# The queries of four heads, moved from the head loop to the seven-product stage by way of DRAM

## The chip, the cores and the metric

The kernel runs on one core of a Trainium2 chip. The metric is the device time of one execution in microseconds (us): 1060.2 us is the median of three runs of the kernel before (1059.62 to 1060.6). The profile shown here comes from one further execution, which took 1058.51 us, 1056.7 us of it between its first and its last instruction (the span).

## The reference, cut to what matters

One layer with three parallel branches, merged by gates, then a feed-forward part. 640 tokens (512 sample, 128 prompt), model width 1024. All branches and gates take their inputs from one projection z = h @ w_in. The change concerns the first 512 columns of z, `zq`, from which the queries of four heads come.

```python
h = rms_norm(x, p['norm_mix']) * (1 + scale1) + shift1
z = h @ p['w_in']                       # 640 x 1024 times 1024 x 7168
zq, zf_f, zf_b, zi, zg, zu, zv, zp, zgate = jnp.split(z, offsets, axis=-1)
# hgrn2_mixer: 4 heads of 128
q = (jax.nn.silu(zq) * HG_DK ** -0.5)   # silu(x) = x * sigmoid(x)
f = lb + (1 - lb) * sigmoid(zf); k = 1 - f        # per direction d
o_d = gated linear recurrence of q, k, v = zi with decay f
o_hg = rms_norm(o_0 + o_1, norm_gain) * silu(zg)
merged = g_hg * (o_hg @ w_branch_hg) + g_sg * (o_sg @ w_branch_sg) + g_pool * (o_pool @ w_branch_pool)
```

## The kernel before, in words

Every projection is done in three matmuls for one product: both operands are split into a high and a low part (`split`, L124 to L127: ScalarE copies the high part, VectorE subtracts it to get the low part), and `mm3` (L193 to L198) multiplies high by high, high by low and low by high. The transposed input stands as `hx` (`h1h`, `h1l`), 8 slices of 128 features by 640 tokens, which are treated as two halves of 320. A block of z is 128 columns: 128 x 640 results.

TensorE's (PE's) instructions stand in program order; what the other engines and the DMA queue of SyncE (SP) run is put in order by a scheduler when the program is built, and each queue is then served strictly in that order.

There are two ways to make blocks of z.

The z stage (`z_pair`, L570) makes two blocks at a time from seven half-size products, in the manner of Strassen and Winograd: each of the seven is 4 slices x 3 matmuls of 128 x 320. It needs sums of the weights (`pair_forms`, L542) and of the inputs, which VectorE makes, and three evacuations and additions at the end. Each pair's weights are prepared during the pair before. The iterator `zpairs` (L538) says which columns come in which order: two pairs for the spatial branch (ZU), four pairs of gates, then pooling and more gates. Each pair's last product runs in the next pair (`pending`).

The head loop makes single blocks in the plain way (`z_cols`, L809, which calls `by_halves`, L798): for each half of the tokens 8 slices x 3 matmuls into one PSUM bank, of which there are three (`ps_mm`). `head_inputs` (L853) makes four such blocks for each head: the query Q (`silu`, L876), two forget gates (FF, FB) and the output gate (ZG). The weights of these blocks come in the order of `plan` (L170), two units ahead at least.

The recurrence of each head (`head`, L893) is a chain of small steps in which PE, VectorE and ScalarE take turns: a product of keys and queries (`scores`) for 32 tokens near each other, then seven levels, each with `scores`, a product on VectorE that updates `xq` in place, and another that updates `xk`, then transposes of the keys (`kt`), state updates (`upd`, then `sf` and `sb` on VectorE), the output product (`o`), its norm, and a transpose (`ot`) whose result is split into `oh`. These steps are strewn among the blocks' matmuls by a count of ticks: `tick()` (L208) is called after every two slices, that is after 6 matmuls, and a step that says `yield n` lets n ticks pass before the next one is written into PE's program:

```python
    LEVEL_TICKS = (3, 3, 3, 3, 2, 2, 2)
    ...
        yield 3              # before the first scores
        yield LEVEL_TICKS[n] # before the scores of level n
        yield 2              # before kt
        yield 2              # before upd
        yield 3              # before o
        yield 6              # before ot
```

That is 34 ticks for each head. A block in the head loop gives 8 ticks. The heads run one after another, each as soon as its inputs and the head before it are done. After the four heads' inputs `HG_ORDER` (L168) lists the rest: six gate blocks ("g", 8 ticks each), then the products of the branch's output with `w_branch_hg` ("b", which read `oh` of all four heads, head by head) mixed with two more gates. Ahead of the first "b" stands `drain()` (L1042), which writes all steps that are not yet in PE's program one behind the other.

Of the kernel before, what the change touches and what calls it, by code (L numbers as in the profile page):

```python
# [9 lines left out]
F32 = mybir.dt.float32  # L10
F32R = mybir.dt.float32r
I32 = mybir.dt.int32
AF = mybir.ActivationFunctionType
ALU = mybir.AluOpType
PSUM = bass.MemoryType.PSUM

P = 128
D = 1024
KD = D // P
TS, TP = 512, 128  # L20
T = TS + TP
NT = T // P
HALF = T // 2
# [7 lines left out]
NH = 4  # L31
# [4 lines left out]
OFF_Q, OFF_FF, OFF_FB, OFF_ZI, OFF_ZG, OFF_ZU, OFF_ZV, OFF_ZP, OFF_GATE = (  # L36
    0, 512, 1024, 1536, 2048, 2560, 3072, 3584, 4096)
# [28 lines left out]
def block_kernel(ctx: ExitStack, tc, x_prompt, x_sample, state, w_ada, w_in, w_bhg, w_bsg,  # L66
# [3 lines left out]
    nc = tc.nc  # L70
    ctx.enter_context(tc.manual_schedule(engines={mybir.EngineType.PE}))

    def pool(stack, name, bufs=1, space=None, side="left"):
        kw = {"side": side}
        if space is not None:
            kw = {"space": space}
        return stack.enter_context(tc.tile_pool(name=name, bufs=bufs, reuse_waits="tile", **kw))
# [7 lines left out]
    dram = ctx.enter_context(tc.tile_pool(name="dram", bufs=1, space=bass.MemoryType.DRAM))  # L85
# [67 lines left out]
    def cols_unit(w, c0, nk=KD):  # L153
        return (w, ((c0, P),), 0, nk)

    def rows_unit(w, n, q):
        return (w, ((n * 512, 512),), 2 * q, 2)

    def unit_parts(u):
        w, spans, k0, nk = u  # L160
        at, parts = 0, []
        for c0, n in spans:
# [5 lines left out]
    HG_ORDER = ([("g", j) for j in range(6)]  # L168
                + [("b", 0), ("b", 1), ("b", 2), ("g", 6), ("b", 3), ("b", 4), ("b", 5), ("g", 7), ("b", 6), ("b", 7)])
    plan = ([rows_unit(w_in, OFF_ZI // 512, q) for q in range(4)]  # L170
            + [cols_unit(w_in, c + h * P) for h in range(NH) for c in (OFF_Q, OFF_FF, OFF_FB, OFF_ZG)]
            + [cols_unit(w_in, OFF_GATE + j * P) if what == "g" else cols_unit(w_bhg, j * P, NH)
               for what, j in HG_ORDER]
            + [rows_unit(w_out, n, q) for n in range(2) for q in range(4)]
# [18 lines left out]
    def mm3(out, ws, xs, first, last, more=False):  # L193

        (wh, wl), (xh, xl) = ws, xs
        nc.tensor.matmul(out, lhsT=wh, rhs=xh, start=first, stop=False, skip_group_check=more)  # L196
        nc.tensor.matmul(out, lhsT=wh, rhs=xl, start=False, stop=False, skip_group_check=more)  # L197
        nc.tensor.matmul(out, lhsT=wl, rhs=xh, start=False, stop=last, skip_group_check=more)  # L198
# [4 lines left out]
    def later(n, fn):  # L203
        at = now[0] + n
        i = sum(d <= at for d, _ in due)
        due.insert(i, (at, fn))

    def tick():  # L208
        now[0] += 1
        while due and due[0][0] <= now[0]:  # L210
            due.pop(0)[1]()
# [106 lines left out]
    hx = (hpool.tile([P, KD, T], F32R, name="h1h"), hpool.tile([P, KD, T], F32R, name="h1l"))  # L318
    qscr = dram.tile([P, 2, HK, HALF], F32, name="qscr")
    vscr = dram.tile([P, NT, 512], F32, name="vscr")  # L320


    junk = spool.tile([P, D], F32, name="junk")
# [148 lines left out]
    zk = pool(zst, "zk", side="right")  # L472
# [25 lines left out]
    def q_tile():  # L498
        return ps_q.tile([P, 512], F32, tag="q", name="q")[:, 0:HALF]
# [30 lines left out]
    def branch_operand(pl, name):  # L530
# [4 lines left out]

    zpairs = iter([OFF_ZU, OFF_ZU + 2 * P] + [OFF_GATE + D + j * P for j in range(0, KD, 2)]  # L538
                  + [OFF_ZP + 2 * P, OFF_GATE + 2 * D, OFF_ZP]
                  + [OFF_GATE + 2 * D + j * P for j in range(2, KD, 2)])  # L540

    def pair_forms():  # L542
        c0 = next(zpairs, None)
        if c0 is None:
            yield None
        raws = [wraw(unit_parts(cols_unit(w_in, c)), KD) for c in (c0, c0 + P)]
        a11, a12, a21, a22 = (half_of(r, n) for r in raws for n in range(2))
        sm = zk.tile([P, HK * P], F32, tag="s", name="s", bufs=1)[:].rearrange("p (k c) -> p k c", k=HK)
        nc.vector.tensor_tensor(sm, a21, a22, op=ALU.add)
        nc.vector.tensor_tensor(a21, a21, a11, op=ALU.add)  # L550
        f = {}

        def put(ws, *names):
            for n, name in enumerate(names):
                f[name] = tuple(half_of(w, n) for w in ws)

        put(wsplit(raws[0]), "A11", "A12")
        nc.vector.tensor_tensor(a11, a11, sm, op=ALU.add)
        nc.vector.tensor_tensor(a12, a12, a11, op=ALU.add)
        ws = wpool.tile([P, 1024], F32R, tag="w", name="ws", bufs=WBUFS)[:].rearrange("p (k c) -> p k c", k=KD)  # L560
        f["s"] = half_of(ws, 0), half_of(ws, 1)
        split(*f["s"], sm)
        put(wsplit(raws[0]), "t", "u")
        yield f
        put(wsplit(raws[1]), "w", "A22")
        yield f
# [3 lines left out]
    def z_pair(done, extra=()):  # L570


        f = made.pop()
        extra = list(extra) + [lambda: None] * 2

        def product(bank, what, xs, first=False):
            for k in range(HK):
                mm3(bank, tuple(w[:, k, :] for w in f[what]), tuple(x[:, k, :] for x in xs),
                    first and k == 0, k == HK - 1, not first)
                if k % 2 == 1:  # L580
                    tick()

        a, b = q_tile(), q_tile()
        product(a, "A11", z11, True)
        product(b, "A12", z21, True)
        while pending:
            pending.pop(0)()
        g0, g1 = (zk.tile([P, T], F32, tag="u", name="z", bufs=7) for _ in range(2))
        ev = [zk.tile([P, HALF], F32, tag="ev", name="ev", bufs=3)[:] for _ in range(3)]
        nc.scalar.activation(ev[0], a, AF.Copy)  # L590
        c = q_tile()
        product(c, "s", zq1, True)
        forms = pair_forms()
        nc.scalar.activation(ev[1], c, AF.Copy)
        nc.vector.tensor_tensor(g0[:, 0:HALF], b, ev[0], op=ALU.add)
        product(a, "t", zq2)
        nc.scalar.activation(ev[2], a, AF.Copy)
        following = next(forms)
        extra[0]()
        product(c, "u", z22)  # L600
        if following:
            next(forms)
            made.append(following)
        nc.vector.tensor_tensor(g0[:, HALF:], c, ev[2], op=ALU.add)
        product(a, "w", zt3)
        nc.vector.tensor_tensor(g1[:, HALF:], a, ev[1], op=ALU.add)
        done(0, g0)
        extra[1]()

        def rest():  # L610
            product(a, "A22", zq4)
            done(1, g1, a)

        pending.append(rest)
# [26 lines left out]
    for g0 in (0, 2):  # L641
        def gelu_done(n, u, a=None, g0=g0):
            gelu(n, u, a)
            later(6, lambda: spatial(g0 + n, u))

        z_pair(gelu_done)

    def pool_out(g, pooled):
        px = px_tile()
        for h, to, z0, n in ((0, 0, ZA, HALF), (1, 0, ZA + HALF, TS - HALF), (1, TS - HALF, ZB, TP)):  # L650
            nc.tensor.matmul(px[:, h, to:to + n], lhsT=pw[:, g, :], rhs=pooled[:, z0:z0 + n], start=True, stop=True)
        nc.scalar.activation(halves(opl[0][:, g, :]), px[:, :, 0:HALF], AF.Copy, scale=par("pool_scale", g))
        nc.vector.scalar_tensor_tensor(halves(opl[1][:, g, :]), px[:, :, 0:HALF], par("pool_scale", g),
                                       halves(opl[0][:, g, :].bitcast(F32)), op0=ALU.mult, op1=ALU.subtract)
# [198 lines left out]
    def head_inputs(h):  # L853
        q = hz.tile([P, T], F32, tag="q", name="q", bufs=1)
        tot = hz.tile([P, 2, T], F32, tag="tot", name="tot", bufs=2)
        xk = hz.tile([P, 2, T], F32, tag="xk", name="xk", bufs=2)
        gz = hz.tile([P, T], F32, tag="gz", name="gz", bufs=2)

        def sig():
            return hz.tile([P, T], F32, tag="sig", name="sig", bufs=2)  # L860

        def forget(c0, d):
            at = slice(d * NH + h, d * NH + h + 1)
            sgs = [sig() for _ in range(2)]
            to = (tot[:, 1 - d, :], 1.0, lb[:, at]), (xk[:, d, :], -1.0, 0.0)

            def done(t, ps):
                for sg, (x, sign, bias) in zip(sgs, to):
                    nc.scalar.activation(sg[:, t], ps, AF.Sigmoid, scale=sign)
                if t.stop == T:  # L870
                    for sg, (x, sign, bias) in zip(sgs, to):
                        nc.scalar.activation(x, sg[:], AF.Identity, scale=lb1[:, at], bias=bias)

            z_cols(c0, done)

        def silu(c0, dst, scale):  # L876
            sg = sig()

            def done(t, ps):
                nc.scalar.activation(sg[:, t], ps, AF.Sigmoid)  # L880
                nc.vector.scalar_tensor_tensor(dst[:, t], ps, scale, sg[:, t], op0=ALU.mult, op1=ALU.mult)

            z_cols(c0, done)

        silu(OFF_Q + h * P, q, float(P) ** -0.5)
        if h == 0:
            nc.sync.dma_start(v[:], vscr[:])
        forget(OFF_FF + h * P, 0)
        forget(OFF_FB + h * P, 1)
        silu(OFF_ZG + h * P, gz, 1.0)  # L890
        return q, tot, xk, gz
# [659 lines left out]
    with tc.manual_schedule(engines={mybir.EngineType.Activation, mybir.EngineType.DVE, mybir.EngineType.Pool}):  # L1551
        ready = None
        for i in range(NT):
            for q, (c, ps) in enumerate(pss[i]):
# [3 lines left out]
                c = slice(512 + c.start, 512 + c.stop)  # L1558
# [97 lines left out]
```

## Time and profile before

| | |
|---|---|
| median of three runs | 1060.2 us (1059.62 to 1060.6) |
| profiled execution | 1058.51 us, span 1056.7 us |
| PE busy | 1034.5 us, 98% |
| VectorE (DVE) busy | 729.8 us, 69% |
| ScalarE (ACT) busy | 525.7 us, 50% |
| GpSimd (POOL) busy | 43.2 us, 4% |
| share of PE in the chain that ended last | 95% |

The stages on the time axis: inputs, norm and the first two projections to about 92 us, the z stage to about 303 us, the head loop with the six gates behind it to 520 us, the "b" products and gates to about 552 us, then the output projection and the feed-forward part. A matmul's duration in the trace overlaps with its neighbours', so the time of a matmul in a dense row is the distance between two starts. The granted TensorE clock has two levels, 1.00 (2.4 GHz) and 0.50 (1.2 GHz) in the profile's rows.

### The profile page before, as it was taken

The numbers are of one execution on the slowest core, as the hardware profiler recorded it, in microseconds if no ns is written. First come the engines' busy times: TensorE is split into PE (matmuls) and PEld (weight loads), VectorE is DVE, ScalarE is ACT, GpSimd is POOL, SyncE is SP. The second block draws the span as 40 slices with busy tenths as digits, with TensorE's granted clock in tenths as the row PEclk, the third lists the DMA queues.
The fourth block names the chain that finished last, engine by engine and source line by source line (L and its number), as shares of the span: only waits on it lengthen the run. The fifth ranks groups of instructions, "written<-read, shape, count | busy, mean of one in ns | idle before, by whom it ended". The sixth has DMA issues, their size and how long they took to land.

```text
span 1056.7 us, 19815 instructions
## 1 busy us (share of the span) xinstructions
PE 1034.5 (98%) x8230; PEld 964.2 (91%) x8230; DVE 729.8 (69%) x1119; ACT 525.7 (50%) x917; POOL 43.2 (4%) x111
## 2 busy tenths in 40 slices
PE   6999999999999999999999999999999999999997
PEld 4789999999999899898998899999999999888886
DVE  5486955697345665756465588999999998845634
ACT  5575644355225545543332366566666666634432
POOL 1030000000000000000000110000000000000201
PEclk9999999999999999999999999999999999999999
DMA  9964323232293544533236421222323223722202
GB/s 292 323 215 130 93 82 96 62 90 61 78 285 106 186 125 145 168 98 115 95 111 199 120 83 58 80 81 83 98 81 99 81 80 101 265 94 60 80 1 100
DMA packets 151770, 126.74 MB, mean 120 GB/s; under 512 B 4832, under 2 KB 132208, under 8 KB 151168
## 3 DMA queue, kind: packets, MB, share of 16 engines
q1 hardware_dynamic: 150960, 124.17, 38.4%
q8 instruction: 64, 1.05, 0.4%
q10 hardware_dynamic: 720, 1.31, 0.3%
q14 instruction: 26, 0.21, 0.1%
HBM read 114.96 MB, written 10.50 MB: 119 GB/s over the span
## 4 chain that ended last, share of the span: by engine, by line
PE 95%; DMA 1%; DVE 1%; ACT 1%; issue 1%; SPq 0%; POOL 0%; POOLq 0%; DVEq 0%; ACTq 0%
PE up L196 15%; PE up L198 15%; PE up L197 15%; PE mm L196 7%; PE mm L198 6%; PE mm L197 6%; PE q L196 5%; PE q L198 5%; PE q L197 5%; PE scores L912 2%; PE px L196 1%; PE px L198 1%; PE px L197 1%; PE ada L280 1%; PE zv L196 1%; PE zi L198 1%
## 5 line engine op out<-in xcount | busy, mean ns | idle before, releaser
L127 DVE TENSOR_TENSOR wl<-raw,wh 128x1024 fp32r<-128x1024 f32 (+1 forms) x105 | 123.9, 1182 | 91.7 <-ACT wh L126 34.4
L126 ACT ACTIVATE wh<-raw 128x1024 fp32r<-128x1024 f32 (+1 forms) x105 | 107.2, 1022 | 56.9 <-PE q L197 21.9
L196 PE MATMUL mm<-h1h,wh 128*128 128x320 f32 x384 | 123.5, 322 | 0.0
L198 PE MATMUL mm<-h1h,wl 128*128 128x320 f32 x384 | 118.7, 309 | 0.0
L197 PE MATMUL mm<-h1l,wh 128*128 128x320 f32 x384 | 118.6, 309 | 0.0
L197 PE MATMUL up<-wl,ah 128*128 128x512 f32 (+1 forms) x242 | 89.8, 371 | 0.0
L196 PE MATMUL up<-wh,ah 128*128 128x512 f32 (+1 forms) x242 | 89.7, 371 | 0.0
L198 PE MATMUL up<-wh,ah 128*128 128x512 f32 (+1 forms) x242 | 89.6, 370 | 0.0
L1198 ACT ACTIVATE wh<-raw 128x1024 fp32r<-128x1024 f32 x62 | 65.1, 1050 | 45.9 <-DVE raw L1189 43.6
L196 PEld LDWEIGHTS mm<-h1h,wh 128*128 128x128 f32 x384 | 72.1, 188 | 13.2 <-issue 12.8
L1203 DVE TENSOR_TENSOR wl<-raw,wh 128x1024 fp32r<-128x1024 f32 x62 | 75.6, 1220 | 8.4 <-ACT wh L1198 8.4
L197 PEld LDWEIGHTS mm<-h1l,wh 128*128 128x128 f32 x384 | 72.2, 188 | 0.0
L198 PEld LDWEIGHTS mm<-h1h,wl 128*128 128x128 f32 x384 | 72.1, 188 | 0.0
L126 ACT ACTIVATE ah<-act 128x512 fp32r<-128x512 f32 x88 | 35.9, 461 | 64.1 <-PE up L198 62.3
L127 DVE TENSOR_TENSOR ah<-act,ah 128x512 fp32r<-128x512 f32 x88 | 38.8, 487 | 32.5 <-ACT ah L126 32.5
L196 PE MATMUL q<-h1h,wh 128*128 128x320 f32 x192 | 59.7, 311 | 0.0
L198 PE MATMUL q<-h1h,wl 128*128 128x320 f32 x192 | 59.4, 309 | 0.0
L197 PE MATMUL q<-h1l,wh 128*128 128x320 f32 x192 | 59.4, 309 | 0.0
L196 PEld LDWEIGHTS up<-wh,ah 128*128 128x128 f32 x242 | 45.6, 189 | 7.8
L198 PEld LDWEIGHTS up<-wh,ah 128*128 128x128 f32 x242 | 45.6, 188 | 7.8
L197 PEld LDWEIGHTS up<-wl,ah 128*128 128x128 f32 x242 | 45.6, 189 | 7.8
L1278 DVE SCALAR_TENSOR_TENSOR acc<-u,pk,acc 128x643 f32<-128x643 f32 x48 | 42.4, 886 | 2.9 <-ACT acc L1272 2.0
(386 smaller groups left out, 2910.0 us busy)
## 6 DMA issues: line engine op xcount, KB each, us to landing
raw<-in_w_in SPq DMA_DIRECT2D x56, 512.0 KB, 4.3
raw<-in_ffn_up SPq DMA_DIRECT2D x44, 512.0 KB, 3.9
raw<-in_w_ada SPq DMA_DIRECT2D x32, 512.0 KB, 4.5
raw<-in_ffn_down SPq DMA_DIRECT2D x22, 512.0 KB, 3.7
raw<-in_w_ada SPq DMA_DIRECT2D x32, 256.0 KB, 6.1
raw<-in_w_out SPq DMA_DIRECT2D x8, 512.0 KB, 4.8
x2scr<-x SPq DMA_DIRECT2D x5, 512.0 KB
x<-x2scr SPq DMA_DIRECT2D x1, 2560.0 KB
```

Of the source, the lines that this page charges most:

```text
L126: nc.scalar.activation(hi, src, AF.Copy)
L127: nc.vector.tensor_tensor(lo, src, hi.bitcast(F32), op=ALU.subtract)
L196: nc.tensor.matmul(out, lhsT=wh, rhs=xh, start=first, stop=False, skip_group_check=more)
L197: nc.tensor.matmul(out, lhsT=wh, rhs=xl, start=False, stop=False, skip_group_check=more)
L198: nc.tensor.matmul(out, lhsT=wl, rhs=xh, start=False, stop=last, skip_group_check=more)
L280: nc.tensor.matmul(ps[tile_, 0:n // 4], lhsT=cs[:, k0 + k, :], rhs=w[:, g], start=(k0 + k == 0), stop=(k0 + k == KD - 1), tile_position=(0 ...
L912: nc.tensor.matmul(px[rows, i, to(g)], lhsT=ck[:, i * P + g * B:i * P + (g + 1) * B], rhs=rhs(i, g), start=True, stop=True, tile_position= ...
L1198: nc.scalar.activation(hi, src, AF.Copy)
L1203: nc.vector.tensor_tensor(lo, src, hi.bitcast(F32), op=ALU.subtract)
L1278: nc.vector.scalar_tensor_tensor(o, x, w, o, op0=ALU.mult, op1=ALU.add)
```

## The change

The four Q blocks leave the head loop. Two more pairs stand in `zpairs` behind the two ZU pairs; a new function `query_pair` makes them, with sigmoid, product and scale, and writes each finished 128 x 640 block to a scratch buffer in DRAM, `zscr`. In `head_inputs` a DMA from `zscr` into the tile `q` (one buffer) takes the place of `silu(OFF_Q ...)`. `plan` loses the four Q units. The ticks, `LEVEL_TICKS`, `HG_ORDER` and the place of `drain()` stay.

```diff
@@ plan
-            + [cols_unit(w_in, c + h * P) for h in range(NH) for c in (OFF_Q, OFF_FF, OFF_FB, OFF_ZG)]
+            + [cols_unit(w_in, c + h * P) for h in range(NH) for c in (OFF_FF, OFF_FB, OFF_ZG)]
@@ scratch
+    zscr = dram.tile([P, NH, T], F32, name="zscr")
@@ z stage
-    zpairs = iter([OFF_ZU, OFF_ZU + 2 * P] + [OFF_GATE + D + j * P for j in range(0, KD, 2)]
+    zpairs = iter([OFF_ZU, OFF_ZU + 2 * P, OFF_Q, OFF_Q + 2 * P] + [OFF_GATE + D + j * P for j in range(0, KD, 2)]
...
+    def query_pair(h0):
+
+        def done(n, z, a=None):
+            sign = (1.0, -1.0)[n]
+            if n:
+                nc.scalar.activation(z[:, 0:HALF], a, AF.Copy)
+            sg = zk.tile([P, T], F32, tag="u", name="sg", bufs=7)
+            nc.scalar.activation(sg[:], z[:], AF.Sigmoid, scale=sign)
+            nc.vector.scalar_tensor_tensor(z[:], z[:], sign * float(P) ** -0.5, sg[:], op0=ALU.mult, op1=ALU.mult)
+            nc.sync.dma_start(zscr[:, h0 + n, :], z[:])
+
+        z_pair(done)
+
+    for h0 in (0, 2):
+        query_pair(h0)
@@ head_inputs
-        silu(OFF_Q + h * P, q, float(P) ** -0.5)
+        nc.sync.dma_start(q[:], zscr[:, h, :])
```

On PE the end of the last head is where the program reads differently. Before, from the scores of level 5 on (`mm` is a block's product, `kt` the key transposes, `upd` the state updates):

```order
L912 MATMUL scores<-xq,ck 32x64 x20
L280 MATMUL ada<-raw,cs 32x256 x4
L196 MATMUL mm<-h1h,wh 128x320
L197 MATMUL mm<-h1l,wh 128x320
L198 MATMUL mm<-h1h,wl 128x320
...
L965 MATMUL kt<-ident,xk 128x128 x8
L196 MATMUL mm<-h1h,wh 128x320
L197 MATMUL mm<-h1l,wh 128x320
L198 MATMUL mm<-h1h,wl 128x320
```

In the changed kernel, from the scores of level 4 of the last head, the last step with a block's matmuls ahead of it:

```order
L198 MATMUL mm<-h1h,wl 128x320
L929 MATMUL scores<-xq,ck 32x32 x20
L280 MATMUL ada<-raw,cs 32x256 x4
L929 MATMUL scores<-xq,ck 32x64 x20
L280 MATMUL ada<-raw,cs 32x256 x4
L929 MATMUL scores<-xq,ck 32x64 x20
L280 MATMUL ada<-raw,cs 32x256 x4
L982 MATMUL kt<-ident,xk 128x128 x8
L990 MATMUL upd<-v,kt 128x128 x8
L1006 MATMUL o<-v,at 128x128
```

The 102 block matmuls that stood among these steps (12, 12, 12, 12, 18 and 36 of them from the scores of level 4 to `ot`) stand earlier in PE's program now; from the scores of level 4 to `ot` nothing stands between the steps. The other heads keep their 34 ticks.

On SP's queue the start of the head loop, before (`v` is the values' read, `sf` and `sb` are the first head's states):

```order
L134 DMA raw<-in_w_ada 128x1024 x3
L887 DMA v<-vscr 128x2560
L898 DMA sf_3482<-in_state 128x128
L899 DMA sb_3489<-in_state 128x128
L134 DMA raw<-in_w_in 128x8x128 x4
```

and in the changed kernel:

```order
L134 DMA raw<-in_w_ada 128x1024 x3
L902 DMA q<-zscr 128x640
L904 DMA v<-vscr 128x2560
L915 DMA sf_3687<-in_state 128x128
L916 DMA sb_3694<-in_state 128x128
L134 DMA raw<-in_w_in 128x8x128 x3
L902 DMA q<-zscr 128x640
L134 DMA raw<-in_w_ada 128x1024 x2
```

The first query comes in ahead of `v`, the second behind three weight units; each later one waits on the queue for the head before it to have read its own.

## Rows read from the trace of the kernel before

**Rows 1.** Page, part 1: busy us, share of the span, instructions.
```profile
PE 1034.5 (98%) x8230; PEld 964.2 (91%) x8230; DVE 729.8 (69%) x1119; ACT 525.7 (50%) x917; POOL 43.2 (4%) x111
```

**Rows 2.** Waits of PE, whole span: us in total, times, longest.
```profile
PE px L196 <- DVE z L716: 3.1, 2, 2.7
```

**Rows 3.** Stretches of z stage and last head: us, busy by engine, PEclk, DMA, GB/s.
```profile
130.00:292.00 162.00, 159.50 (x1081) 158.36 (x1079) 102.55 (x163) 68.78 (x112) 0.00 (x0) 1.00 0.28 82
...
471.00:517.00 46.00, 46.00 (x649) 41.15 (x648) 24.46 (x43) 17.98 (x40) 1.36 (x2) 1.00 0.33 105
```

**Rows 4.** Chain that ended last, z stage: start us, us, what.
```profile
109.14 1.11 PE px L629 x10
...
123.68 1.11 PE px L629 x10
```

**Rows 5.** PE timeline, end of the last head: start us, us, what.
```profile
489.36 0.31 PE L198 MATMUL mm<-h1h,wl 128*128 128x320 f32 x1
489.60 0.53 PE L912 MATMUL scores<-xq,ck 128*32 128x32 f32 x38
...
492.48 0.77 PE L912 MATMUL scores<-xq,ck 128*32 128x64 f32 x40
...
495.56 0.77 PE L912 MATMUL scores<-xq,ck 128*32 128x64 f32 x40
...
501.19 1.95 PE L973 MATMUL upd<-v,kt 128*128 128x128 f32 x16
...
505.62 0.38 PE L989 MATMUL o<-v,at 128*128 128x128 f32 x2
...
508.43 0.40 PE L196 MATMUL mm<-h1h,wh 128*128 128x320 f32 x1
...
513.80 0.71 PE L1004 MATMUL ot<-ident,o 128*128 128x128 f32 x5
514.26 0.39 PE L196 MATMUL mm<-h1h,wh 128*128 128x320 f32 x1
```

**Rows 6.** DVE timeline, the same stretch, idle before in brackets.
```profile
490.20 0.82 DVE L949 TENSOR_TENSOR xq<-xq,tot 128x640 f32<-128x640 f32 x1
...
502.28 1.11 DVE L976 SCALAR_TENSOR_TENSOR sf<-sf,tot,upd 128x128 f32<-128x128 f32 x3 [0.34 <-PE upd L973]
503.31 1.11 DVE L980 SCALAR_TENSOR_TENSOR sb<-sb,tot,upd 128x128 f32<-128x128 f32 x3
511.68 0.82 DVE L999 TENSOR_TENSOR o<-o,rso 128x640 f32<-128x640 f32 x1 [7.25 <-POOL rso L122]
...
514.54 0.88 DVE L1006 SCALAR_TENSOR_TENSOR og__5968<-ot,pk,gz 128x640 f32<-128x640 f32 x1 [0.88 <-PE ot L1004]
516.23 0.83 DVE L127 TENSOR_TENSOR ohgl<-og__5968,ohgh 128x640 fp32r<-128x640 f32 x1 [0.80 <-ACT ohgh L126]
```

**Rows 7.** ACT timeline, the same stretch.
```profile
496.40 0.70 ACT L944 ACTIVATE at<-scores 128x640 f32<-128x640 f32 x1 [0.29 <-PE scores L912]
497.13 1.37 ACT L947 ACTIVATE at<-near 32x160 f32<-32x160 f32 x4
499.19 1.09 ACT L967 ACTIVATE kt<-kt 128x512 f32<-128x512 f32 x2 [0.69 <-PE kt L965]
...
508.71 0.28 ACT L996 ACTIVATE o<-o 128x128 f32<-128x128 f32 x1 [3.93 <-PE o L989]
...
515.46 0.74 ACT L126 ACTIVATE ohgh<-og__5968 128x640 fp32r<-128x640 f32 x1 [0.96 <-DVE og__5968 L1006]
```

**Rows 8.** Page, part 5: the weights' low parts: busy us, mean ns, idle before.
```profile
L127 DVE TENSOR_TENSOR wl<-raw,wh 128x1024 fp32r<-128x1024 f32 (+1 forms) x105 | 123.9, 1182 | 91.7 <-ACT wh L126 34.4
```

**Rows 9.** Stretches at the program's end, where PE has finished: columns as in rows 3.
```profile
1049.00:1050.00 1.00, 0.33 (x3) 0.13 (x2) 0.89 (x3) 0.56 (x2) 0.00 (x0) 1.00 0.00 0
...
1051.50:1052.00 0.50, 0.00 (x0) 0.00 (x0) 0.10 (x1) 0.10 (x1) 0.36 (x1) 0.98 0.09 25
1052.00:1053.00 1.00, 0.00 (x0) 0.00 (x0) 0.65 (x1) 0.62 (x1) 0.00 (x0) 0.50 0.00 0
```

## The prediction

> **What bounds the kernel now.** I read the page's busy shares first: PE is busy for 98% of the span, no other engine for more than 69% [rows 1]. Then PE's waits: the whole list beyond the start and the tail holds one place that matters, 3.1 us before the head loop, where VectorE is late with a product [rows 2]. Then the stretches: the z stage keeps PE busy for 159.5 of 162 us, the last head for 46.00 of 46 [rows 3]. So before the change the time is PE's program, row after row; what leaves it is gained at full price, and what makes PE wait is lost at full price. Last the timelines of the last head on three engines [rows 5 to 7], since the diff leaves its ticks alone while it takes away the matmuls that the ticks count.
>
> **Part 1: PE's work.** Between the starts of two `px` groups of one z pair lie 123.68 - 109.14 = 14.54 us with two such groups of 1.11 us and the pair's 84 matmuls: 12.32 / 84 = 0.1467 us for one [rows 4]; the last head's pitch is the same. Four Q blocks are 4 x 48 = 192 matmuls, two pairs 2 x 84 = 168. 24 fewer: -3.5 us.
>
> What the pairs add elsewhere I cost at nothing. On VectorE a query pair has the sums and low parts of any pair, and two products of the size of the `og` row, 0.88 us each [rows 6]; it has no `px` product or branch weights. The stage has VectorE at 102.55 of 162 us and ScalarE at 68.78 [rows 3], and weights are made during the pair before. If that cover failed, PE would wait for about one low part a pair, 1.2 us [rows 8], so 0 to +2.4 us. I see no way to below nothing. The four writes to DRAM stand on SP ahead of later weight reads, and each waits for VectorE's product; those reads serve a pair that starts a pair, 12.3 us, later. I take 0, at worst the same 2.4 us.
>
> The read of `q` has a head's whole input time (24 ticks, over 21 us at 6 x 0.1467 each) to land before the first product that needs it. Each later one waits on SP until the head before has read its query; behind it stand weight reads of units that are at least two blocks of 7 us away. I take 0.
>
> **Part 2: the ticks.** A head needs 34 ticks. Before, its inputs gave 4 x 8 = 32: the heads start at ticks 33, 67, 101 and 135, the last ends at 169, and the drain comes at 4 x 32 + 6 x 8 = 176. Nothing is left to drain but a few ticks of slack. After, a head's inputs give 24: the heads start at 25, 59, 93 and 127, and the drain comes at 4 x 24 + 48 = 144, when the last head has done 17 of 34 ticks. Its steps due at 19, 21, 23, 25, 28 and 34 (scores of levels 5 and 6, `kt`, `upd`, `o`, `ot`) are written one behind the other. The 102 matmuls that stood between are done sooner, so they are not lost, but they no longer cover anything, and the first "b" product needs the last head's `oh`.
>
> How long is that chain bare? From the start of the level-4 scores (0):
> - VectorE first makes a low part whose buffer the block just ended has freed, 1.2 us [rows 8], then updates `xq`, 0.82 [rows 6], and hands over in 0.04 (from `og`'s end at 515.42 to `ohgh` at 515.46 [rows 6, 7]): level 5 at 2.05.
> - scores to next engine 0.84 (495.56 to 496.40 [rows 5, 7]), `xq` 0.86: level 6 at 3.75.
> - ScalarE: `at` starts at 4.6, the near copies 0.73 later, and take 1.37; half of the `kt` copies, 0.55 [rows 7]: `upd` at 7.25.
> - `sf` 1.09 after `upd`'s start, `sb` 1.03 later, 1.11 long [rows 5, 6]: 10.5.
> - `o`: 13 pieces in 508.43 - 505.62 = 2.81 us [rows 5]; two are done before `sb` is, eleven remain: 12.9.
> - squares 0.28 later, then 2.97 to the product with the norm (508.71 to 511.68), which hands to `ot` after 0.86 [rows 5 to 7]: 17.0.
> - `og` 0.74, `ohgh` 0.92, `ohgl` 0.77, and 0.87 to PE: 20.3.
>
> PE's own work in it: 514.26 - 489.60 = 24.66 us less 102 x 0.1467 = 14.96, so 9.7 us [rows 5], and ten matmuls of the first "b" half (heads 0 to 2 and one more), 1.5 us. The rest is idle: 20.3 - 9.7 - 1.5 = +9.1 us.
>
> Bounds for the unseen bare chain: without the low part in front, and with the `kt` copies ahead of the near copies, 17.7 us, idle 6.5; at most as long as it was with its matmuls between, 516.23 + 0.83 - 489.60 = 27.5 us, idle 16.3 [rows 5, 6]. I take 20.3, as each step has a row of its own size.
>
> **Part 3: the clock.** Between `o` and `ot` PE would stand for 4.1 us (12.9 to 17.0). At the program's end the granted clock is 1.00 until just before 1052, some 2.6 us after the last matmul, and 0.50 from there on [rows 9]; a wait of 2.7 us at 290 us did not bring it down [rows 2, 3]. So it probably falls once here. At 1.2 GHz `ot` (0.46 us, 513.80 to 514.26 [rows 5]) takes as long again, the ten matmuls still fit ahead of `ohgl`, and some of the following "b" products run at half speed until it rises: 0 to 3 us, I take +1.0 in all.
>
> The Trainium skill (TensorE: Matmul & The Clock Gate, section on HAM oscillation) says that waits between bursts of matmuls bring the clock back to half rate, and that each burst then starts slow. By that rule the term of 1.0 stands, and it speaks for the second rival below; without it the sum would be 1.0 us lower. The fall in the last rows agrees with it.
>
> **The sum.** -3.5 + 9.1 + 1.0 = +6.6 us. From the profiled execution's own 1058.5 us that is 1065.1; the median of the runs shown stands 1.7 us above that execution, and I put the change on the median: 1060.2 + 6.6 = 1066.8 us.
>
> **Rivals.**
> - *The clock is at half through most of the drain.* Between the steps PE does small products with gaps of 1 to 2 us, so the clock could go already at `kt`. Then `upd`, `o` and `ot` on the chain take twice as long (0.9, 2.4 and 0.5 us more) and some 3 us of "b" products too: about 5 us on top, 1072. For it: the fall in rows 9. Against: PE is dense until the level-4 scores, and none of those gaps is as long as the 2.7 us that left the clock alone. The page named above would allow it.
> - *Heads that hold their buffers (slower still).* The inputs now run ahead of the heads by ten ticks a head. The last head's `xk` is written at tick 80, and its buffer is freed by the second head's `kt`, at tick 82; behind that wait on ScalarE stand this head's second `kt` copy and the next block's sigmoids. Three PSUM banks let PE go on for eight ticks, so I cost it at 0; three such places at one 0.9 us tick each would give 1069.5.
> - *VectorE becomes the bound of the query pairs.* Then 2.4 us of the gain go: 1069.2. Against it is its load in the stage.
> - *The other side: the bare chain is nearly covered.* With VectorE and ScalarE free of block work, the last head's steps follow each other so fast that PE idles less than the 3.5 us saved; it decides from a chain of 14.7 us downward (9.7 + 1.5 + 3.5). At no idle at all the time is 1056.7. Against it: its own rows give 17.7 at least.
>
> **How the numbers follow.** Forecast 66%, its own range 1063 to 1070; half clock 13%; held buffers 10%; VectorE 5%; the chain covered 6%. A measurement of this kernel tells about 0.2% from no change, 2.1 us: slower means above 1062.3, faster below 1058.1. Slower holds the first four but for a small part of the forecast's lower edge: 0.89. Of the covered chain most gives faster: 0.05; same 0.06. The range that holds 8 in 10 goes from 1062.5, just under the short chain (1063.2 with no clock loss), to 1073, the long chain without a clock loss and the half clock.
>
> **What would show it.** Right: PE busy without a gap in the z stage, 24 fewer 320-column matmuls; `scores` rows of the last head's levels 4 to 6 within 4 us; a new PE wait of some 4 us before `ot` (for VectorE's `o`), ones of 1 to 3 us before `upd` and `o`, and one for `ohgl` at the first "b" product, 9 us together; a granted clock of 0.50 for a few us behind it. Wrong: no such waits; waits of PE between 92 and 130 us or at the heads' `scores`; or idle time on PE under 3.5 us between levels 4 and "b".

## The result, and the profile after

The changed kernel takes 1066.0 us (median of four runs, 1065.4 to 1066.47), the kernel before 1059.91 us in the runs beside it and those shown above (four, 1057.96 to 1060.6). The ratio is 1.006, with a 95% interval of 1.0047 to 1.0073: slower by 6.1 us. The profiled execution took 1065.4 us, 1063.6 of it span, 6.9 us more than the span before.

Busy shares, the first part of the page of the changed kernel; they answer to [rows 1]:

```profile
PE 1034.3 (97%) x8206; PEld 963.6 (91%) x8206; DVE 740.4 (70%) x1133; ACT 532.8 (50%) x925; POOL 43.0 (4%) x111
```

PE issues 24 matmuls fewer (8230 to 8206) and is busy as long as before. Either the matmuls saved nothing, or others take longer; the rows below show that it is the second. PE's waits over the whole span (us in total, times, longest), which answer to [rows 2]:

```profile
PE ot L1021 <- DVE o L1016: 4.0, 1, 4.0
...
PE px L196 <- DVE z L733: 2.3, 1, 2.3
PE scores L929 <- DVE xq L966: 1.9, 2, 1.1
PE upd L990 <- ACT kt L984: 1.4, 1, 1.4
...
PE o L1009 <- DVE sb L997: 0.9, 1, 0.9
```

The wait at `px` was there before. The other four are new, 8.2 us together, and all lie in the end of the last head. Here is that end on PE (start us, us, what, in brackets the idle time before); it answers to [rows 5]:

```profile
506.22 0.53 PE L929 MATMUL scores<-xq,ck 128*32 128x32 f32 x38
...
508.29 0.77 PE L929 MATMUL scores<-xq,ck 128*32 128x64 f32 x40 [1.07 <-DVE xq L966]
...
510.28 0.77 PE L929 MATMUL scores<-xq,ck 128*32 128x64 f32 x40 [0.79 <-DVE xq L966]
...
511.41 1.09 PE L982 MATMUL kt<-ident,xk 128*128 128x128 f32 x8
513.88 2.05 PE L990 MATMUL upd<-v,kt 128*128 128x128 f32 x16 [1.38 <-ACT kt L984]
...
517.27 0.49 PE L1009 MATMUL o<-sb,xq 128*128 128x128 f32 x2 [0.89 <-DVE sb L997]
...
519.61 0.39 PE L1006 MATMUL o<-v,at 128*128 128x128 f32 x2
524.00 1.33 PE L1021 MATMUL ot<-ident,o 128*128 128x128 f32 x5 [4.01 <-DVE o L1016]
524.98 0.61 PE L196 MATMUL mm<-ohgh,wh 128*128 128x320 f32 x1
...
525.66 0.47 PE L198 MATMUL mm<-ohgh,wl 128*128 128x320 f32 x1
525.93 0.47 PE L196 MATMUL mm<-ohgh,wh 128*128 128x320 f32 x1
...
527.94 0.64 PE L197 MATMUL mm<-ohgl,wh 128*128 128x320 f32 x1
...
529.97 0.33 PE L198 MATMUL mm<-ohgh,wl 128*128 128x320 f32 x1
530.14 0.31 PE L196 MATMUL mm<-ohgh,wh 128*128 128x320 f32 x1
```

The steps follow each other with nothing between. From `ot` on PE works at half pace: `ot` to the next matmul takes 0.98 us where it took 0.46 [rows 5], and the "b" products have a pitch of 0.27 us (525.66 to 525.93), where it is 0.147 at full speed. Stretches of the changed kernel (us, busy by engine, then PEclk, DMA share, GB/s), which answer to [rows 3] and, for the clock, to [rows 9]:

```profile
142.00:305.00 163.00, 163.00 (x1108) 162.36 (x1107) 106.41 (x163) 72.31 (x117) 0.00 (x0) 1.00 0.28 80
340.00:480.00 140.00, 140.00 (x1953) 125.44 (x1953) 86.81 (x140) 69.82 (x140) 3.53 (x4) 1.00 0.50 154
506.00:523.00 17.00, 9.86 (x196) 7.73 (x195) 7.57 (x18) 6.78 (x22) 1.28 (x2) 1.00 0.33 109
506.00:531.00 25.00, 16.86 (x225) 14.39 (x225) 10.60 (x22) 7.51 (x23) 1.36 (x2) 0.86 0.25 86
523.00:524.00 1.00, 0.00 (x0) 0.00 (x0) 0.82 (x1) 0.00 (x0) 0.09 (x1) 0.59 0.70 287
524.00:524.50 0.50, 0.50 (x3) 0.50 (x4) 0.00 (x0) 0.00 (x0) 0.00 (x0) 0.50 0.00 0
529.50:530.00 0.50, 0.50 (x4) 0.50 (x4) 0.00 (x0) 0.00 (x0) 0.00 (x0) 0.50 0.00 0
530.00:531.00 1.00, 1.00 (x8) 1.00 (x8) 0.00 (x0) 0.00 (x0) 0.00 (x0) 1.00 0.02 8
```

The z stage, now with the query pairs, keeps PE busy all the time, and so do the heads from 340 to 480 us. In the 25 us of the last head's end PE stands idle for 8.1. The granted clock is 1.00 through the four shorter waits, falls during the long one, some 3 us after the last `o` matmul, and is back at 1.00 by 530 us, after `ot` and 5 us of "b" products with hardly a pause.

VectorE in the same stretch, which answers to [rows 6]:

```profile
506.18 1.23 DVE L127 TENSOR_TENSOR wl<-raw,wh 128x1024 fp32r<-128x1024 f32 x1 [0.16 <-PE mm L197]
507.32 0.82 DVE L966 TENSOR_TENSOR xq<-xq,tot 128x640 f32<-128x640 f32 x1
...
523.12 0.82 DVE L1016 TENSOR_TENSOR o<-o,rso 128x640 f32<-128x640 f32 x1 [5.91 <-POOL rso L122]
525.37 0.88 DVE L1023 SCALAR_TENSOR_TENSOR og__6036<-ot,pk,gz 128x640 f32<-128x640 f32 x1 [1.42 <-PE ot L1021]
527.06 0.83 DVE L127 TENSOR_TENSOR ohgl<-og__6036,ohgh 128x640 fp32r<-128x640 f32 x1 [0.80 <-ACT ohgh L126]
```

The weight's low part does stand in front of the first `xq`, as the chain of the prediction had it, and `og` comes 1.37 us after the start of `ot` instead of 0.74. ScalarE (ACT) ahead of `upd`, which answers to [rows 7]:

```profile
511.84 1.37 ACT L964 ACTIVATE at<-near 32x160 f32<-32x160 f32 x4
513.23 1.09 ACT L984 ACTIVATE kt<-kt 128x512 f32<-128x512 f32 x2
```

The near copies do stand ahead of the `kt` copies, for 1.4 us, though PE waits for the latter alone.

### The profile page after: what moved, and what is told of

Read it like the earlier page. It is cut to its first block, busy times and chain, and to the rows that moved or that the text cites. A ratio compares the mean times of both kernels' runs of the same rounds, so it can differ in the third digit from the quotient of the medians.

```text
span 1063.6 us, 19823 instructions
## 1 busy us (share of the span) xinstructions
PE 1034.3 (97%) x8206; PEld 963.6 (91%) x8206; DVE 740.4 (70%) x1133; ACT 532.8 (50%) x925; POOL 43.0 (4%) x111
## 4 chain that ended last, share of the span: by engine, by line
PE 49%; DVE 1%; ACT 1%; issue 0%; POOL 0%; POOLq 0%; ACTq 0%
PE up L196 15%; PE up L198 15%; PE up L197 15%; PE mm L197 1%; PE mm L196 1%; PE mm L198 1%; PE up L1150 0%; ACT wh L1215 0%; ACT o L1013 0%; PE ot L1021 0%; DVE wl L1220 0%; POOL rso L122 0%; PE upd L990 0%; PE o L1009 0%; DVE sb L997 0%
## 5 line engine op out<-in xcount | busy, mean ns | idle before, releaser
L127 DVE TENSOR_TENSOR wl<-raw,wh 128x1024 fp32r<-128x1024 f32 (+1 forms) x107 | 126.3, 1183 | 86.1 <-ACT wh L126 39.2
L196 PE MATMUL mm<-h1h,wh 128*128 128x320 f32 x320 | 102.9, 322 | 0.0
L198 PE MATMUL mm<-h1h,wl 128*128 128x320 f32 x320 | 98.9, 309 | 0.0
L197 PE MATMUL mm<-h1l,wh 128*128 128x320 f32 x320 | 98.8, 309 | 0.0
L196 PE MATMUL up<-wh,ah 128*128 128x512 f32 (+1 forms) x242 | 89.6, 370 | 0.0
L196 PEld LDWEIGHTS mm<-h1h,wh 128*128 128x128 f32 x320 | 60.1, 188 | 11.9 <-issue 11.1
L196 PE MATMUL q<-h1h,wh 128*128 128x320 f32 x224 | 69.5, 310 | 0.0
L197 PE MATMUL q<-h1l,wh 128*128 128x320 f32 x224 | 69.2, 309 | 0.0
L198 PE MATMUL q<-h1h,wl 128*128 128x320 f32 x224 | 69.2, 309 | 0.0
L197 PEld LDWEIGHTS mm<-h1l,wh 128*128 128x128 f32 x320 | 60.2, 188 | 0.0
L198 PEld LDWEIGHTS mm<-h1h,wl 128*128 128x128 f32 x320 | 60.1, 188 | 0.0
L196 PEld LDWEIGHTS up<-wh,ah 128*128 128x128 f32 x242 | 45.6, 188 | 7.8
```

The lines of the kernel that those rows point to most:

```text
L127: nc.vector.tensor_tensor(lo, src, hi.bitcast(F32), op=ALU.subtract)
```

## The experiments

Each kernel was timed in turn with the kernel before; ratios are to that. The first two ask whether the loss has the place and the cause that the prediction gave it; then it is halved, and taken away in two ways; the last asks what the clock is worth.

**The pairs alone.** The heads still make their own queries, so that their ticks are those of before; the pairs' queries go to DRAM and are not read.

```diff
-            + [cols_unit(w_in, c + h * P) for h in range(NH) for c in (OFF_FF, OFF_FB, OFF_ZG)]
+            + [cols_unit(w_in, c + h * P) for h in range(NH) for c in (OFF_Q, OFF_FF, OFF_FB, OFF_ZG)]
-        nc.sync.dma_start(q[:], zscr[:, h, :])
+        silu(OFF_Q + h * P, q, float(P) ** -0.5)
```

Expected: 

> The first part of the change alone: the two query pairs are made in the z stage and written to DRAM, but the heads still make their own queries in the loop and do not read the pairs' (so 168 matmuls of 128x320 are done for nothing). The ticks are as in the kernel before. Theory (the pairs cost PE's work and nothing else, and the read by way of DRAM has no part in the loss): 1059.6 + 168 x 0.1467 = 1059.6 + 24.6 = 1084.2 us, no wait of PE in the z stage, none in the last head's end. Rival (VectorE or the writes hold PE up in the query pairs): 2.4 us more, 1086.7, with waits of PE between 115 and 150 us. Rival (the loss is not from the ticks but from the z stage or the transfer): 1090 or more.

Measured: 1083.43 us (four runs, 1082.23 to 1084.08) beside 1060.4; ratio 1.0212 (1.0197 to 1.0227), that is +22.5 us (20.9 to 24.1). Its stretches of the query pairs (their sigmoids run from 126 to 146 us) and of the last head's end:

```profile
112.00:142.00 30.00, 30.00 (x212) 30.00 (x211) 25.39 (x42) 17.32 (x26) 0.00 (x0) 1.00 0.36 109
...
516.00:545.00 29.00, 29.00 (x291) 27.78 (x291) 9.81 (x21) 9.95 (x28) 1.36 (x2) 1.00 0.22 72
```

VectorE is at 25.4 of 30 us in the query pairs, so it has little to spare there, but PE never waits for it. With the ticks back, the end of the last head has no wait. The sum of 24.6 us lies half a microsecond above the interval; the wait at `px`, 3.1 us before and 2.3 here, is more than that. The first part of the change costs PE its matmuls and no more than that. This kernel does not read the queries back; that the reads cost nothing is seen in the changed kernel, where PE has no gap from 340 to 480 us.

**The drain alone, in the kernel before.** Nothing of the queries is changed; three gate blocks stand ahead of the first "b" instead of six, so that the drain comes at tick 4 x 32 + 3 x 8 = 152, with the last head at tick 17 of 34, as in the changed kernel.

```diff
-    HG_ORDER = ([("g", j) for j in range(6)]
-                + [("b", 0), ("b", 1), ("b", 2), ("g", 6), ("b", 3), ("b", 4), ("b", 5), ("g", 7), ("b", 6), ("b", 7)])
+    HG_ORDER = ([("g", j) for j in range(3)] + [("b", 0), ("b", 1), ("b", 2)]
+                + [(what, j) for j in range(3, 8) for what in ("g", "b")])
...
-        if n == 6:
+        if n == 3:
             drain()
```

Expected: 

> The kernel before, queries in the head loop, with three gate blocks instead of six ahead of the drain (the other five follow among the b products): the drain comes at tick 152 with the last head at tick 17 of 34, as in the changed kernel, and the same PE work in all. Theory: the same waits of 8 us and the half clock behind them, with nothing saved: 1060 + 11 = 1071 us, 1069 to 1073. Rival A (pairs of the z stage or buffers make the loss, not the drain): 1060 to 1062.

Measured: 1070.32 us (four runs, 1068.68 to 1071.22) beside 1059.64; ratio 1.010 (1.0085 to 1.0115). Its waits of PE:

```profile
PE ot L1004 <- DVE o L999: 4.0, 1, 4.0
...
PE scores L912 <- DVE xq L949: 1.9, 2, 1.1
PE upd L973 <- ACT kt L967: 1.4, 1, 1.4
...
PE o L992 <- DVE sb L980: 0.9, 1, 0.9
```

These are the changed kernel's waits, to the tenth, in a kernel without the change, and here too the granted clock is 0.50 behind the longest (508 to 513 us). It lies 10.7 us above before (9.0 to 12.2), the changed kernel 6.1: the difference is the 3.5 us of matmuls that only the latter saves, within the intervals.

**Half the dose.** The changed kernel with seven gates ahead of the drain (tick 152; the last head is at tick 25 of 34).

```diff
-    HG_ORDER = ([("g", j) for j in range(6)]
-                + [("b", 0), ("b", 1), ("b", 2), ("g", 6), ("b", 3), ("b", 4), ("b", 5), ("g", 7), ("b", 6), ("b", 7)])
+    HG_ORDER = ([("g", j) for j in range(7)]
+                + [("b", 0), ("b", 1), ("b", 2), ("b", 3), ("b", 4), ("b", 5), ("g", 7), ("b", 6), ("b", 7)])
...
-        if n == 6:
+        if n == 7:
```

Expected: 

> The changed kernel with seven gate blocks ahead of the drain instead of six, and the seventh "b" where the seventh gate stood. The last head is then at tick 25 of 34 when the drain comes: the steps up to upd have their matmuls again, only o and ot are bare. Theory (the bare chain is the loss, step by step): the waits before scores and upd (1.9 and 1.4 us) go, those before o and ot (0.9 and 4.0 us) stay, so 1066.0 - 3.3 = 1062.7 us. On the clock: if the 4 us wait before ot alone brings it down, the granted clock is 0.50 behind it as in the changed kernel; if the row of shorter waits ahead of it was needed, it stays at 1.00 and the time is another 1 to 1.6 us lower, 1061.1 to 1061.7. Rival (one fixed price for any drain ahead of the head's end): no less than 1065.

Measured: 1062.91 us (twelve runs, 1061.26 to 1064.87) beside 1060.4; ratio 1.0025 (1.0014 to 1.0035). Two of its waits, and two of its stretches:

```profile
PE ot L1021 <- DVE o L1016: 3.9, 1, 3.9
...
PE o L1009 <- DVE sb L997: 0.9, 1, 0.9
```

```profile
526.00:527.00 1.00, 0.00 (x0) 0.00 (x0) 0.16 (x1) 0.00 (x0) 0.80 (x1) 0.90 1.07 451
...
532.00:533.00 1.00, 1.00 (x5) 1.00 (x5) 0.41 (x1) 0.00 (x0) 0.00 (x0) 0.50 0.00 0
```

The waits before `scores` and `upd` are gone, the other two unchanged, and the time falls by 3.1 us, near the 3.3 that the lost waits measured. The clock falls in the wait of 3.9 us as before, though PE was dense up to `upd` and only the 0.9 us before `o` stood ahead of it: the row of shorter waits was not needed for that.

**The cover back, by blocks.** All eight gates ahead of the drain (tick 160 of 161).

```diff
-    HG_ORDER = ([("g", j) for j in range(6)]
-                + [("b", 0), ("b", 1), ("b", 2), ("g", 6), ("b", 3), ("b", 4), ("b", 5), ("g", 7), ("b", 6), ("b", 7)])
+    HG_ORDER = [("g", j) for j in range(8)] + [("b", j) for j in range(8)]
...
-        if n == 6:
+        if n == 8:
```

Expected: 

> The changed kernel with all eight gate blocks ahead of the drain and the eight b products behind it: 160 ticks for the heads, which end at 161. Theory (the bare end of the last head costs 8.1 us of PE waits and some 3 us of half clock): the waits before the level scores, upd, o and ot go; only ot's result is late for the first b product, by about 2 us; near 1057.5 us, 1056 to 1059. Rival A (the loss lies in the pairs of the z stage or in heads that hold their buffers): stays at 1066 or rises, since b products without gate blocks between them load VectorE. Rival B (the waits go, but eight b products in a row make PE wait for VectorE and ScalarE): PE waits of 3 us or more behind the heads, 1059 to 1063.

Measured: 1057.31 us (eleven runs, 1055.72 to 1059.36) beside 1059.64; ratio 0.9981 (0.9972 to 0.999). It puts back the cover, and it also leaves no gates among the "b" products. Of the four waits none is left; in their place are two short ones at the first "b" product, for the split of the last head's output (its file is a line shorter, so L195 is L196 elsewhere):

```profile
PE mm L196 <- DVE ohgl L127: 0.4, 1, 0.4
PE mm L195 <- ACT ohgh L126: 0.4, 1, 0.4
```

**The cover back, by the ticks.** The order of blocks as in the changed kernel; a head takes 29 ticks instead of 34, so that the last head is done at tick 24 + 4 x 29 + 1 = 141, ahead of the drain at 144.

```diff
-    LEVEL_TICKS = (3, 3, 3, 3, 2, 2, 2)
+    LEVEL_TICKS = (3, 3, 2, 2, 2, 2, 2)
...
-        yield 3              # before the first scores
+        yield 2
...
-        yield 3              # before o
+        yield 2
...
-        yield 6              # before ot
+        yield 5
```

Expected: 

> The changed kernel with 29 ticks a head in place of 34 (2 before the first scores, levels 3, 3, 2, 2, 2, 2, 2, then 2, 2, 2 and 5): the heads end at tick 141, the drain stays at 144. Theory: the drain is empty, and a bare level took 2.0 us in the changed kernel's drain against 2.9 us that two ticks and the step's own work give, so the shorter steps hide as before: about 1056 us, 1055 to 1057.5. Rival A (heads that hold their buffers make the loss): the heads free them sooner, so some gain, but 1060 or more with waits where the blocks are written. Rival C (the shorter steps do not hide): PE waits at scores and o of each head, four times 1 to 2 us: 1060 to 1064.

Measured: 1055.96 us (six runs, 1055.35 to 1057.81) beside 1059.64; ratio 0.9966 (0.9954 to 0.9978), that is -3.6 us, the fastest of all the kernels here and faster than both that this text compares. Five ticks fewer a head cost one wait of 0.4 us:

```profile
PE px L196 <- DVE z L733: 2.6, 1, 2.6
...
PE scores L929 <- DVE kd L922: 0.4, 1, 0.4
```

So the change does hold the 3.5 us of its matmuls, and the end of the last head took them and 6 us more. What 29 ticks a head would do to the kernel before was not run; its last head keeps PE busy for 46.00 of 46 us [rows 3], so little is to be had there.

**The clock alone.** In the changed kernel 26 matmuls whose results nobody reads fill the wait before the last `ot`.

```diff
+        if h == NH - 1:
+            warm = ps_mm.tile([P, 512], F32, tag="mm", name="warm")[:, 0:HALF]
+            for i in range(26):
+                nc.tensor.matmul(warm, lhsT=hx[0][:, 0, 0:P], rhs=hx[0][:, 0, 0:HALF], start=True, stop=True)
```

Expected: 

> The changed kernel with 26 matmuls of 128 x 320 into a bank that nobody reads, put between o and ot of the last head, 3.8 us in a wait of 4.0 us: work added, nothing removed. Theory (half clock behind the long wait costs about 3 us): the granted clock stays at 1.00, ot takes 0.5 instead of 1.0 us and the following products 0.147 instead of 0.267 us each: 2 to 3 us faster, 1063 to 1064.5. Rival D (the half clock costs nothing, since PE waits there anyway): 1066 or slightly more.

Measured: 1066.72 us (five runs, 1064.57 to 1067.04) beside 1059.64; ratio 1.006 (1.0046 to 1.0074), no less than the changed kernel's: a miss. On PE:

```profile
508.91 0.77 PE L929 MATMUL scores<-xq,ck 128*32 128x64 f32 x40 [1.06 <-DVE xq L966]
...
520.37 4.06 PE L1013 MATMUL warm<-h1h 128*128 128x320 f32 x26
524.62 0.77 PE L1025 MATMUL ot<-ident,o 128*128 128x128 f32 x5 [0.19 <-DVE o L1020]
...
527.13 0.42 PE L196 MATMUL mm<-ohgh,wh 128*128 128x320 f32 x1 [0.42 <-ACT ohgh L126]
527.99 0.41 PE L197 MATMUL mm<-ohgl,wh 128*128 128x320 f32 x1 [0.44 <-DVE ohgl L127]
```

```profile
520.00:525.00 5.00, 4.81 (x35) 4.55 (x34) 0.82 (x1) 1.51 (x10) 1.36 (x2) 1.00 0.56 213
```

The clock stays up (1.00, behind the same four shorter waits), but the ten "b" matmuls that run ahead of `ohgl` are done sooner only to wait for it. From the scores of level 5 to the first product with `ohgl` it is 19.08 us here and 19.65 in the changed kernel; behind it seven matmuls at half speed took 2.03 us where they need 1.03. So the trace gives the clock 1.6 us in this place. The profiled execution lost most of that elsewhere: from the end of its wait at `px` to the first block of the head loop it took 12.2 us (315.40 to 327.57), the changed kernel 10.7 (316.24 to 326.91). This stretch of it, and then the same of the changed kernel:

```profile
315.00:320.00 5.00, 4.60 (x21) 4.63 (x22) 1.60 (x4) 1.06 (x1) 0.00 (x0) 0.66 1.15 306
```

```profile
315.00:320.00 5.00, 3.76 (x26) 3.79 (x27) 2.43 (x4) 0.12 (x1) 0.00 (x0) 1.00 1.15 315
```

A half-speed stretch there comes in one profiled execution and not in the other. With it the profiled execution is still 0.9 us shorter than the changed kernel's (span 1062.7 against 1063.6). The timed runs can't tell a gain of 1.6 us from none: two of the five took 1064.6 us and three 1066.7 to 1067.0, and each of the two ratios to the kernel before (both 1.006) is known to some 1.4 us. What made the three longer stays open. It was not more time at half speed, as their mean granted clock (0.997 and 0.998) is no lower than in the two shorter runs (0.997 and 0.995).

## Why the prediction was right

It said 1066.8 us, and 1066.0 was measured, for the reason given. Point by point:

- *PE's work, -3.5 us.* 24 instructions fewer, a dense z stage, and -3.6 us in the version whose last head is covered. That the pairs, their writes and the reads cost nothing held too: PE has no wait at all between 60 and 300 us.
- *The ticks, +9.1 us.* The mechanism is shown: the same four waits come up without the change when the drain is moved, shrink with the dose and vanish with the cover. The size was near. PE's idle time is 8.1 to 8.2 us, but the chain is longer than foreseen: counted from the level-4 scores (506.22), the steps come at 2.07, 4.06, 7.66, 11.05, 17.78 and 21.72 us, where the prediction had 2.05, 3.75, 7.25, 10.5, 17.0 and 20.3. Against the same 11.2 us of PE's own work at full speed the chain costs 21.7 - 11.2 = 10.5 us; of the 2.3 that aren't idle in it some 1.7 are half-speed work (`ot` and the ten "b" matmuls), which stands where the wait for `ohgl` was expected.
- *The clock, +1.0 us.* It fell once, in the wait before `ot`, for about 6.7 us. Of the chain's 1.4 us of excess 0.63 is `ot` at half speed (`og` after 1.37 instead of 0.74 us), and the seven matmuls behind the chain add 1.0: 1.6 in all by the trace, which the times neither confirm nor rule out. In the prediction's own terms the ticks are then 10.5 - 0.6 = +9.9 us and the clock +1.6.
- *The sum.* -3.5 + 10.5 + 1.0 makes +8.0; the wait at `px` is 0.8 us shorter than before, which the forecast did not have. It goes with the pairs: the two kernels without them in the z stage have 3.1 and 3.3 us there, the six with them 2.3 to 2.6; by what way, no run shows. That gives +7.2, against +6.9 between the spans and +6.1 between the medians. Two terms were a little too small and a small gain was missed, and that the forecast came closer than its parts is luck.
- *The signs.* Two did not come out as they were written. The wait for `ohgl` is not there, for the reason above. And waits at the heads' `scores` stand among the signs of being wrong, while the prediction's own chain requires them: levels 4 to 6 come 2.05 and 1.7 us apart, and PE has 1.0 to 1.2 us of work in each. They came, 1.9 us, in the last head alone.

The rivals: the half clock through most of the drain fell, since the stretch from 506 to 523 us has a granted clock of 1.00. (Its price was added up short too: 0.9 + 2.4 + 0.5 + 3 less the 1.0 that the sum already has is 5.8 us, not 5.) Held buffers fell: no wait in the other heads, and no loss when the last head is covered. VectorE as the bound of the query pairs fell with the dense rows of the pairs. The covered chain fell with 8 us of idle time, 4.6 more than it allowed.

The Trainium skill (TensorE: Matmul & The Clock Gate, section on HAM oscillation) has waits bring PE back to half rate and the next burst start slow. The "b" products behind the wait of 4.0 us agree (0.50). `upd` and `o`, behind waits of 1.4 and 0.9 us, ran at 1.00, so the rival of the half clock through the drain, which the prediction calls the second though it is the first of its list, did not come. The section's case is one of waits longer than the bursts between them, and these were shorter (1.4 us behind 2.2 us of work), so it spoke less for that rival than the prediction has it.

## What to carry to other kernels

Where small steps are strewn among other work by a count of that work, the count is a schedule: work taken out elsewhere takes the cover from the steps that come last. Before such a change, count the ticks that are left at the point where everything must be done, and price what stands bare there by the durations of its steps; here that gave 9.1 us for the bare end, where the trace has 9.9 by the same count. Then retune the counts along with the change: five ticks fewer for each head turned a loss of 0.6% into a gain of 0.3%.

## What the runs showed of the hardware

- What a half-speed stretch cost hung on what stood behind it. Of 17 "b" matmuls at a pitch of 0.27 us, ten only filled a wait that would have been there. Ahead of the head loop nothing waited, and the stretch cost its matmuls whole: 1.5 us with the 26 added matmuls, 2.8 with 29 ticks (13.4 us from the wait's end to the first block, where the changed kernel took 10.7).
- The waits of PE at `px` ahead of the head loop are nearly alike in the profiled executions, yet the granted clock behind them is not, and their length doesn't sort them. It stays at 1.00 behind 2.27 us (the changed kernel), 2.31 (seven gates), 2.54 (eight gates) and 2.71 (the kernel before); over 315 to 320 us it is 0.68 behind 2.31 (the pairs alone), 0.66 behind 2.46 (the 26 added matmuls), and behind 2.62 (29 ticks):

```profile
315.00:320.00 5.00, 3.26 (x12) 3.29 (x13) 2.93 (x4) 0.12 (x1) 0.00 (x0) 0.61 1.15 317
```

- SP's queue stood for up to 6.1 us with a read of `q` at its head, waiting for the head before to have read its own, and PE did not wait once for what was queued behind:

```profile
SPq L902 <- PE scores L929: 12.0, 3, 6.1
```
